# Odd layer's attention: probabilities transposed in 32-row strips, four banks at once

## The chip, the cores and the metric

The kernel runs on one core of a Trainium2 chip, in one launch. The metric is the device time of one execution in microseconds (us); lower is better. The engines are named as the profile names them: PE (TensorE's matmuls), PEld (TensorE's weight loads, which run beside its matmuls), DVE (VectorE), ACT (ScalarE), POOL (GpSimd), SP (SyncE, which issues most DMAs). "Bank" is one of the eight PSUM banks, 128 partitions x 512 float32, into which matmuls write.

## The reference, cut to what is touched

A two-layer encoder on 256 tokens of width 1024. Layer 0 (neighbourhood attention and latent attention) is not touched. Layer 1, the odd one, is attention over three groups of dilated windows, 16 heads of 64, and all three groups share one softmax by way of their denominators:

```python
for gi in range(g):                       # windows (128,1), (512,4), (2048,16)
    sc = einsum('bqhd,bqjhd->bhqj', q[gi], k_sel) * scale, masked
    e = exp(sc - max(sc)); z = sum(e)
    outs.append(einsum('bhqj,bqjhd->bqhd', e / z, v_sel)); lses.append(m + log(z))
out = sum(softmax(lses) * outs)           # then out @ w_o, residual, squared-ReLU MLP
```

## The kernel before, in words

All 256 tokens stay on the chip (two tiles of 128, `NT`); weights stream from HBM and each is split on ACT and DVE into a high and a low part (L177, L178), so that a float32 product becomes passes in the fast format (`mm2` at L187/L188, `mm3` at L181 to L183).

The odd layer works in eight units of two heads. For a unit, `qk_steps` makes queries and keys in 12 steps (three blocks `b`, two features `f`, two halves; each pair of halves fills one bank of the tag `acc`, which `joined` then empties by an ACT copy, L194, and a DVE add, L195), and `all_values` makes values in 4 steps. The attention of earlier units is put between those steps by `beside` and `burst`: the burst that belongs to unit u-1 stands after step 5 of unit u's steps, that is, right behind the product b=1, f=0, and the burst of unit 7 after step 13 of its own steps. What is left (products of units 6 and 7, transposes of unit 7) stands between the steps of the output product.

A burst for unit u has three parts, in this order:

- `mix(u-2)`: sums of values (L956, L961) into one bank, which is then split by ACT (L177) and DVE (L178).
- `turn(u-1)`: PE transposes (L942) of the probabilities `pp`, 128 queries x 384 keys for each token tile i and head j, then copies (L946) from the banks to the tile `pts`.
- `scores(u)`: L202 (two heads beside each other, each on 64 rows of the array) and L920 (four 64 x 64 products beside each other), then the softmax on DVE and ACT (L926 to L930).

Each 128-query block is transposed in two strips of 64 rows, which lie on different rows of the array and write different banks. A unit's 24 transposes stand in two groups of 12, one for each token tile: the first ahead of L202, the second, by the callback `between`, behind it.

Two pools of PSUM tags exist, `acc` and `w`, of four banks each, and each request takes the next bank in turn, so an operation that writes a bank waits until the bank's last user has been emptied. The order of instructions on each engine is fixed when the kernel is built, by a list scheduler that starts from the program's order and may move an instruction that it expects to wait; on the chip every engine works through its own list.

Of the kernel before, what the change touches and what calls it, by code (L numbers as in the profile page):

```python
# [16 lines left out]
F32 = mybir.dt.float32  # L17
# [6 lines left out]
P = 128  # L24
# [3 lines left out]
NT = T // P  # L28
# [17 lines left out]
def trunk(ctx, tc, a, out):  # L46
    nc = tc.nc
# [23 lines left out]
    def quarter_pair(name):  # L71
        return pair_tile(act, KT // 2, name, 2, "quarter")
# [5 lines left out]
    def bank(tag):  # L78
        return ps.tile([P, 512], F32, tag=tag, name=tag)
# [17 lines left out]
    ident = const.tile([P, P], F32, name="ident")  # L97
# [70 lines left out]
    def weight():  # L168

        j = state["used"]  # L170
        prefetch(j + 1, j + 1)
        prefetch(j + LOAD_AHEAD, j + SPLIT_AHEAD)
        state["used"] = j + 1
        return parts.pop(j)[1:]
# [38 lines left out]
    def soon():  # L213

        return tc.high_priority(DRAIN_PRIO)

    def tok(t):
        return slice(t * P, (t + 1) * P)
# [106 lines left out]
    def open_accs():  # L325
        return [bank("acc") for _ in range(4)]

    def onto(accs, w, c, m, first, last, fbs):

        for fb in fbs:  # L330
            cs = slice(c + fb * P, c + fb * P + P)
            o = accs[fb // 2][:, (fb % 2) * T:(fb % 2) * T + T]
            mm3(o, w[0][:, cs], w[1][:, cs], *halves(m), first and fb % 2 == 0, last and fb % 2 == 1)

    def out_steps(accs, mixed, wo, k):

        def step(fbs):
            if k // 2 not in wo:
                wo[k // 2] = weight()
            onto(accs, wo[k // 2], (k % 2) * D, mixed[k // 4][:, k % 4], k == 0, k == KT - 1, fbs)  # L340
        return [lambda fbs=fbs: step(fbs) for fbs in (range(0, 4), range(4, 8))]
# [484 lines left out]
    def odd(op, xT, s):  # L826
# [6 lines left out]
        mixed = [quarter_pair("oa"), quarter_pair("ob")]  # L833
# [72 lines left out]

        probs, turned = {}, {}

        def scores(u, d, between):

            ss = {(i, j): bank("w") for i in range(NT) for j in range(2)}
            for i in range(NT):
                two_heads([ss[i, j][:, 0:T] for j in range(2)], d["q0"], tok(i))
            between()
            for i in range(NT):
                for g in range(2):
                    for c in range(2):
                        for j in range(2):
                            pb, own = slice(64 * j, 64 * j + 64), slice(i * P + 64 * c, i * P + 64 * c + 64)
                            nc.tensor.matmul(ss[i, j][64 * c:64 * c + 64, T + 64 * g:T + 64 * g + 64], d["q12"][pb, g, own],  # L920
                                             d["k12"][pb, g, own], start=True, stop=True)
            for i in range(NT):
                for j in range(2):
                    sn, pp = scratch([384], "sn"), op.tile([P, 384], F32, tag="pp", name="pp", bufs=4)
                    mn, z, rz = (work.tile([P, 1], F32, tag=v, name=v, bufs=4) for v in ("dmn", "dz", "drz"))
                    nc.vector.tensor_tensor_reduce(out=sn, in0=ss[i, j][:, 0:384], in1=mask[:, i, :], op0=ALU.add, op1=ALU.min,  # L926
                                                   scale=-(HD ** -0.5), scalar=3e38, accum_out=mn)
                    nc.scalar.activation(pp, sn, AF.Exp, bias=mn, scale=-1.0, accum_out=z)
                    nc.vector.reciprocal(rz, z)
                    nc.scalar.activation(pp, pp, AF.Copy, scale=rz)  # L930
                    probs[u, i, j] = pp

        def turn(u, i, tag):

            pt = [bank(tag) for _ in range(2)]
            for j in range(2):
                pp = probs.pop((u, i, j))
                for b in range(3):
                    at = slice((3 * j + b) * 64, (3 * j + b) * 64 + 64)
                    for r in range(2):  # L940
                        rows = slice(64 * r, 64 * r + 64)
                        nc.tensor.transpose(pt[r][:, at], pp[rows, b * P:(b + 1) * P], ident[rows, rows])  # L942
            pts = turned[u, i] = op.tile([P, 6, P], F32, tag="pts", name="pts", bufs=2)
            with soon():
                for r in range(2):
                    nc.any.tensor_copy(out=pts[:, :, 64 * r:64 * r + 64], in_=pt[r][:, 0:384].rearrange("p (b n) -> p b n", b=6))  # L946

        def mix(u, d, out_tag):
            pvo = bank(out_tag)
            for i in range(NT):  # L950
                pts = turned.pop((u, i))
                at = i * P
                for kk in range(NT):
                    for j in range(2):
                        cs = slice(64 * j, 64 * j + 64)
                        nc.tensor.matmul(pvo[cs, tok(i)], d["v0"][:, kk, cs], pts[:, 3 * j + kk, :], start=kk == 0, stop=False)  # L956
                for c in range(2):
                    qs = slice(64 * c, 64 * c + 64)
                    for j in range(2):
                        cs = slice(64 * j, 64 * j + 64)  # L960
                        nc.tensor.matmul(pvo[cs, at + 64 * c:at + 64 * c + 64], d["v12"][:, 2 * i + c, cs], pts[:, 3 * j + 2, qs],  # L961
                                         start=False, stop=c == 1)
            with soon():
                split(*halves(mixed[u // 4][:, u % 4]), pvo[:, 0:T])

        units = [unit_tiles(0)]
        d = units[0]
        v0, v_out = value_steps(d)
        run_all(v0)
        r = [rstd(s)]  # L970
# [8 lines left out]
        def beside(main, placed):  # L979

            for i, step in enumerate(main):
                step()
                if i in placed:
                    placed[i]()

        def burst(u):

            def step():
                if u > 1:
                    mix(u - 2, units[u - 2], "acc")  # L990
                if u > 0:
                    turn(u - 1, 0, "acc")
                scores(u, units[u], lambda: turn(u - 1, 1, "acc") if u > 0 else None)
            return step

        for u in range(1, 8):
# [4 lines left out]
            beside(qk_steps(units[u]) + all_values(units[u]), placed)  # L1001
        accs, wo = open_accs(), {}

        def last_turn():
            mix(6, units[6], "w")
            for i in range(NT):
                turn(7, i, "w")

        beside([f for k in range(6) for f in out_steps(accs, mixed, wo, k)], {6: last_turn, 9: lambda: mix(7, units[7], "w")})
        return accs, out_last(accs, mixed, wo)  # L1010

    def phase(name, fn, *args):
# [3 lines left out]
    accs, last = phase("even", even)  # L1016
    xT, s = hand_over(accs, last, 1)
    accs, last, scale = phase("mlp0", mlp_between, xT, s)
    xT, s = hand_over_tokens(accs, last, 2, scale)
    accs, last = phase("odd", odd, xT, s)  # L1020
# [100 lines left out]
```

## Time and profile before

| | |
|---|---|
| runs (3) | 740.52 to 744.68 us, median 742.35 us |
| profiled execution | 740.85 us, its span 739.0 us |
| PE / PEld busy | 99% / 87% of the span |
| DVE / ACT / POOL busy | 73% / 63% / 1% |
| odd layer's units 1 to 7 (bursts) | from 354.0 us to 519.4 us; leftovers to 544.2 us |
| transposes L942 | 192 matmuls of 64 rows x 128 columns, 222 ns each in the record |

Matmuls overlap, so a record of 222 ns is a latency and not a price: what a row of transposes costs is read from the distance between starts, or from the chain of waits, which shows each group by the time that it added. A timeline row "384.55 0.53 ... x12" is a group of 12 that starts at 384.55 and whose last record ends 0.53 later. "64*128" behind a matmul is the part of the array in use, rows x columns.

### The profile page before, as it was taken

What the parts mean: (1) busy time and instruction counts of PE and PEld (TensorE: products, weight loads), DVE (VectorE), ACT (ScalarE), POOL (GpSimd) and SP (SyncE); (2) the same over time, 40 slices, a digit from 0 to 9 for tenths busy, and PEclk for the clock granted to TensorE, in tenths of its full rate; (3) what the DMA queues carried; (4) which work ended last, traced back from release to release, by engine and by line L of the source; (5) the groups of instructions that cost most, each with busy time, mean ns of one, the idle gap of its engine ahead of it and who ended that gap; (6) DMA issues with size and microseconds to landing.
All of it is one profiled execution on the core that took longest, in us unless ns stands there. A gap on an engine that the chain in (4) does not pass through costs nothing.

```text
span 739.0 us, 12836 instructions
## 1 busy us (share of the span) xinstructions
PE 729.3 (99%) x4932; PEld 641.4 (87%) x4932; DVE 538.2 (73%) x1116; ACT 463.5 (63%) x1038; POOL 6.0 (1%) x16
## 2 busy tenths in 40 slices
PE   8999999999999999999999999999999999999996
PEld 6898998888888888989999899898998888888885
DVE  6698869666666666998878888888659665665664
ACT  7689977554554556757768767776757445554541
POOL 0100000000000000000000000000000000000000
PEclk9999999999999999999999999999999999999999
DMA  8966334555555554575573665556345546455501
GB/s 288 345 207 222 116 123 163 197 202 181 178 211 180 178 184 149 200 238 200 191 247 122 200 229 169 195 173 201 128 191 194 206 171 220 168 181 200 178 20 57
DMA packets 28108, 136.89 MB, mean 185 GB/s; under 512 B 4496, under 2 KB 7056, under 8 KB 14992
## 3 DMA queue, kind: packets, MB, share of 16 engines
q1 hardware_dynamic: 27760, 135.81, 53.5%
q8 instruction: 38, 0.62, 0.3%
q10 hardware_dynamic: 288, 0.28, 0.1%
q14 instruction: 22, 0.18, 0.1%
HBM read 127.68 MB, written 1.05 MB: 174 GB/s over the span
## 4 chain that ended last, share of the span: by engine, by line
PE 89%; ACT 4%; DMA 3%; DVE 2%; issue 1%; SPq 1%; POOLq 0%; POOL 0%; ACTq 0%; DVEq 0%
PE w L187 16%; PE acc L181 13%; PE acc L182 13%; PE acc L183 13%; PE acc L187 11%; PE w L188 8%; PE acc L188 6%; PE w L761 1%; DMA raw<-in_w_v 1%; PE w L202 1%; DMA bias<-in_rpb 1%; DVE wlo L178 1%; PE acc L942 1%; PE w L729 1%; PE w L181 1%
## 5 line engine op out<-in xcount | busy, mean ns | idle before, releaser
L178 DVE TENSOR_TENSOR wlo<-raw,whi 128x512 fp32r<-128x512 f32 (+3 forms) x488 | 302.4, 665 | 67.6 <-ACT whi L177 67.2
L177 ACT CAST whi<-raw 128x512 fp32r<-128x512 f32 (+3 forms) x488 | 263.8, 602 | 80.7 <-issue 70.0
L187 PE MATMUL w<-xT,whi 128*128 128x512 f32 x512 | 179.4, 394 | 0.0
L187 PE MATMUL acc<-xT,whi 128*128 128x512 f32 x384 | 134.6, 396 | 0.0
L188 PE MATMUL w<-xT,wlo 128*128 128x256 f32 x512 | 132.8, 280 | 0.0
L187 PEld LDWEIGHTS w<-xT,whi 128*128 128x128 f32 x512 | 93.6, 187 | 18.3
L188 PEld LDWEIGHTS w<-xT,wlo 128*128 128x128 f32 x512 | 96.1, 188 | 5.5
L188 PE MATMUL acc<-xT,wlo 128*128 128x256 f32 x384 | 99.8, 280 | 0.0
L181 PE MATMUL acc<-whi,h 128*128 128x512 f32 x250 | 98.4, 393 | 0.0
L182 PE MATMUL acc<-wlo,h 128*128 128x512 f32 x250 | 97.8, 391 | 0.0
L183 PE MATMUL acc<-whi,h 128*128 128x512 f32 x250 | 97.4, 390 | 0.0
L187 PEld LDWEIGHTS acc<-xT,whi 128*128 128x128 f32 x384 | 69.8, 187 | 13.5
L194 ACT COPY up<-w 128x256 f32<-128x256 f32 x64 | 23.9, 373 | 88.6 <-PE w L187 88.6
L188 PEld LDWEIGHTS acc<-xT,wlo 128*128 128x128 f32 x384 | 72.1, 188 | 3.7
L195 DVE TENSOR_TENSOR up<-up,w 128x256 f32<-128x256 f32 x64 | 26.8, 419 | 62.9 <-ACT up L194 62.1
L181 PE MATMUL acc<-whi,xT 128*128 128x384 f32 (+2 forms) x160 | 56.1, 351 | 0.9 <-ACT whi L177 0.9
L182 PE MATMUL acc<-wlo,xT 128*128 128x384 f32 (+2 forms) x160 | 56.0, 350 | 0.4 <-DVE wlo L178 0.4
L183 PEld LDWEIGHTS acc<-whi,h 128*128 128x128 f32 x250 | 47.0, 188 | 10.2
L182 PEld LDWEIGHTS acc<-wlo,h 128*128 128x128 f32 x250 | 47.0, 188 | 9.8
L183 PE MATMUL acc<-whi,xT 128*128 128x384 f32 (+2 forms) x160 | 55.4, 346 | 0.0
L181 PEld LDWEIGHTS acc<-whi,h 128*128 128x128 f32 x250 | 46.9, 188 | 9.1
L182 PEld LDWEIGHTS acc<-wlo,xT 128*128 128x128 f32 x160 | 30.1, 188 | 3.1 <-DVE wlo L178 2.1
(201 smaller groups left out, 1009.6 us busy)
## 6 DMA issues: line engine op xcount, KB each, us to landing
raw<-in_w SPq DMA_DIRECT2D x64, 1024.0 KB, 4.8
raw<-in_w_oqk SPq DMA_DIRECT2D x24, 1024.0 KB, 5.1
raw<-in_w_ov SPq DMA_DIRECT2D x16, 768.0 KB, 4.6
sw<-qk SPq DMA_DIRECT2D x96, 64.0 KB, 3.6
raw<-in_w_qk SPq DMA_DIRECT2D x4, 1024.0 KB, 10.6
raw<-in_w_oe SPq DMA_DIRECT2D x4, 1024.0 KB, 7.7
raw<-in_w_oo SPq DMA_DIRECT2D x4, 1024.0 KB, 5.8
bias<-in_rpb SPq DMA_DIRECT2D x8, 256.0 KB, 5.3
```

The lines of the kernel that those rows point to most:

```text
L177: a = nc.scalar.copy(hi, src).ins
L178: return a, (eng or nc.vector).tensor_tensor(lo, src, hi.bitcast(F32), op=ALU.subtract).ins
L181: nc.tensor.matmul(o, sh, mh, start=first, stop=False)
L182: nc.tensor.matmul(o, sh, ml, start=False, stop=False)
L183: nc.tensor.matmul(o, sl, mh, start=False, stop=last)
L187: both = lambda: nc.tensor.matmul(o, sh, m.rearrange("p v n -> p (v n)"), start=first, stop=last)
L188: low = lambda: nc.tensor.matmul(o[:, 0:T], sl, m[:, 0, :], start=False, stop=False)
L194: nc.scalar.copy(dst, o[:, T:2 * T])
L195: nc.vector.tensor_tensor(dst, dst, o[:, 0:T], op=ALU.add)
L202: nc.tensor.matmul(o[j], qk[pb, 0, a, ts], qk[pb, 1, b, :], start=n == 0, stop=n == 2)
L729: nc.tensor.transpose(pt[:, b * P:(b + 1) * P], pp[:, b // 2, (b % 2) * P:(b % 2 + 1) * P], ident)
L761: nc.tensor.matmul(pvo[64 * j:64 * j + 64, o + own.start:o + own.stop], v[:, kk, h * 64:(h + 1) * 64], block(2 * j + kk), start=kk == 0, s ...
```

## The change

`turn` now takes a whole unit (both token tiles, both heads) at once, cuts every 128-query block into four strips of 32 rows instead of two of 64, and writes them to four banks, so a unit has 48 transposes of 32 moving columns in place of 24 of 64. They all stand between `mix` and `scores`; the callback goes. `mix` takes its bank from `w` instead of `acc`; `turn` takes all four `acc` banks. `pts` is one tile of 12 blocks in place of two of 6. The four copies of a unit move as many elements as before, in runs of 32 instead of 64. Behind the last unit, `mix(6)` and `turn(7)`, which stood together after step 6 of the output product, now stand after steps 5 and 6.

```diff
@@ -906,12 +906,11 @@
 
         probs, turned = {}, {}
 
-        def scores(u, d, between):
+        def scores(u, d):
 
             ss = {(i, j): bank("w") for i in range(NT) for j in range(2)}
             for i in range(NT):
                 two_heads([ss[i, j][:, 0:T] for j in range(2)], d["q0"], tok(i))
-            between()
             for i in range(NT):
                 for g in range(2):
                     for c in range(2):
@@ -930,25 +929,26 @@
                     nc.scalar.activation(pp, pp, AF.Copy, scale=rz)
                     probs[u, i, j] = pp
 
-        def turn(u, i, tag):
-
-            pt = [bank(tag) for _ in range(2)]
-            for j in range(2):
-                pp = probs.pop((u, i, j))
-                for b in range(3):
-                    at = slice((3 * j + b) * 64, (3 * j + b) * 64 + 64)
-                    for r in range(2):
-                        rows = slice(64 * r, 64 * r + 64)
-                        nc.tensor.transpose(pt[r][:, at], pp[rows, b * P:(b + 1) * P], ident[rows, rows])
-            pts = turned[u, i] = op.tile([P, 6, P], F32, tag="pts", name="pts", bufs=2)
+        def turn(u, tag):
+
+            pt = [bank(tag) for _ in range(4)]
+            for i in range(NT):
+                for j in range(2):
+                    pp = probs.pop((u, i, j))
+                    for b in range(3):
+                        n = (2 * i + j) * 3 + b
+                        for r in range(4):
+                            rows = slice(32 * r, 32 * r + 32)
+                            nc.tensor.transpose(pt[r][:, 32 * n:32 * n + 32], pp[rows, b * P:(b + 1) * P], ident[rows, rows])
+            turned[u] = op.tile([P, 12, P], F32, tag="pts", name="pts", bufs=1)
             with soon():
-                for r in range(2):
-                    nc.any.tensor_copy(out=pts[:, :, 64 * r:64 * r + 64], in_=pt[r][:, 0:384].rearrange("p (b n) -> p b n", b=6))
+                for r in range(4):
+                    nc.any.tensor_copy(out=turned[u][:, :, 32 * r:32 * r + 32], in_=pt[r][:, 0:384].rearrange("p (b n) -> p b n", b=12))
 
         def mix(u, d, out_tag):
             pvo = bank(out_tag)
             for i in range(NT):
-                pts = turned.pop((u, i))
+                pts = turned[u][:, 6 * i:6 * i + 6]
                 at = i * P
                 for kk in range(NT):
                     for j in range(2):
@@ -987,10 +987,10 @@
 
             def step():
                 if u > 1:
-                    mix(u - 2, units[u - 2], "acc")
+                    mix(u - 2, units[u - 2], "w")
                 if u > 0:
-                    turn(u - 1, 0, "acc")
-                scores(u, units[u], lambda: turn(u - 1, 1, "acc") if u > 0 else None)
+                    turn(u - 1, "acc")
+                scores(u, units[u])
             return step
 
         for u in range(1, 8):
@@ -1001,12 +1001,8 @@
             beside(qk_steps(units[u]) + all_values(units[u]), placed)
         accs, wo = open_accs(), {}
 
-        def last_turn():
-            mix(6, units[6], "w")
-            for i in range(NT):
-                turn(7, i, "w")
-
-        beside([f for k in range(6) for f in out_steps(accs, mixed, wo, k)], {6: last_turn, 9: lambda: mix(7, units[7], "w")})
+        beside([f for k in range(6) for f in out_steps(accs, mixed, wo, k)],
+               {5: lambda: mix(6, units[6], "w"), 6: lambda: turn(7, "w"), 9: lambda: mix(7, units[7], "w")})
         return accs, out_last(accs, mixed, wo)
 
     def phase(name, fn, *args):
```

On every engine the order is otherwise as before but for a few rows. Three places matter below.

PE at the burst in unit 1's steps, which has no `mix`: the rows behind the product L187/L188, with the waits for semaphores in brackets. Before:

```order
L187 MATMUL acc<-xT,whi 128x512
L942 MATMUL acc<-ident,pp 128x64 [waits DVE_49,Activation_49]
L942 MATMUL acc<-ident,pp 128x64 [waits DVE_49]
L942 MATMUL acc<-ident,pp 128x64 x10
L202 MATMUL w<-q_3510 128x256 x12
L942 MATMUL acc<-ident,pp 128x64 [waits DVE_49] x2
L942 MATMUL acc<-ident,pp 128x64 x10
L920 MATMUL w<-k_3512,q_3511 64x64 x16
```

The same place now:

```order
L187 MATMUL acc<-xT,whi 128x512
L942 MATMUL acc<-ident,pp 128x32 [waits DVE_49,Activation_49]
L942 MATMUL acc<-ident,pp 128x32 [waits DVE_49] x2
L942 MATMUL acc<-ident,pp 128x32 x24
L942 MATMUL acc<-ident,pp 128x32 [waits DVE_49]
L942 MATMUL acc<-ident,pp 128x32 x20
L202 MATMUL w<-q_3510 128x256 x12
L919 MATMUL w<-k_3512,q_3511 64x64 x16
```

The second group has moved ahead of L202 (L920 is now L919). The transpose that waits for DVE in the middle is the first into the fourth bank, which is the bank of the product just ahead; the scheduler has put 27 transposes of the first three strips before it, and behind it stand 9 of the fourth strip alone, then 12 in turn over all four banks. In the bursts of units 2 to 7 that wait stands at the 8th or 9th of the 48 and the rest follow in turn.

DVE behind the burst of unit 7 (L894 and L899 are the rotary embedding of this unit's keys, which L920 needs). Before:

```order
L178 TENSOR_TENSOR ob<-acc,ob 128x256
L946 COPY pts<-acc 128x6x64
L894 TENSOR_TENSOR sw<-sw,sinT 128x512
L946 COPY pts<-acc 128x6x64
L899 TENSOR_TENSOR k_5792<-r_6090,sw 128x512
```

Now:

```order
L178 TENSOR_TENSOR ob<-w,ob 128x256
L946 COPY pts<-acc 128x12x32 x2
L894 TENSOR_TENSOR sw<-sw,sinT 128x512
L899 TENSOR_TENSOR k_5907<-r_6228,sw 128x512
L925 ISA sn,dmn<-w,mask 128x384
```

Both copies now stand ahead of both steps of the keys.

PE in the output product, where `mix(6)` and `turn(7)` stood together. Before:

```order
L956 MATMUL w<-pts,v_5401 64x128 x4
L961 MATMUL w<-pts,v_5402 64x64 x4
L942 MATMUL w<-ident,pp 128x64 x15
L942 MATMUL w<-ident,pp 128x64 [waits DVE_49]
L942 MATMUL w<-ident,pp 128x64 x8
L181 MATMUL acc<-oa,whi 128x256 [waits Activation_49]
```

Now the sums stand 12 output matmuls ahead, and the transposes alone:

```order
L183 MATMUL acc<-oa,wlo 128x256
L942 MATMUL w<-ident,pp 128x32 x3
L942 MATMUL w<-ident,pp 128x32 [waits DVE_49]
L942 MATMUL w<-ident,pp 128x32 x44
L181 MATMUL acc<-oa,whi 128x256 [waits Activation_49]
```

The wait of the 16th transpose for the split of `mix(6)`'s bank has become a wait of the 4th, a step of the output product later than the sums.

## The prediction

> **What bounds the kernel now.** I read the page first, then who waits for whom on PE in the odd layer.
>
> ```profile
> PE 729.3 (99%) x4932; PEld 641.4 (87%) x4932; DVE 538.2 (73%) x1116; ACT 463.5 (63%) x1038; POOL 6.0 (1%) x16
> ...
> PE 89%; ACT 4%; DMA 3%; DVE 2%; issue 1%; SPq 1%; POOLq 0%; POOL 0%; ACTq 0%; DVEq 0%
> ```
>
> ```profile
> PE acc L181 <- ACT v L864: 0.3, 1, 0.3
> PE w L942 <- DVE ob L178: 0.2, 1, 0.2
> PE acc L942 <- DVE ob L178: 0.2, 1, 0.2
> ```
>
> PE carries 99% of the span and 89% of the chain that ended last. In the 240 us around the odd layer it waits three times, 0.7 us together, and two of these are transposes that wait for a bank. So what the change does to the time is what it does to PE's own time at eight places, and new waits for banks. DVE and ACT are behind PE nearly everywhere.
>
> **What a row of transposes costs.** The chain at one full burst (the one in unit 2's steps), then PE's timeline there, and a burst without transposes (unit 0):
>
> ```profile
> 382.75 0.44 PE acc L956 x8
> 383.19 0.23 PE acc L961 x8
> ...
> 384.71 0.37 PE acc L942 x12
> 385.08 0.62 PE w L920 x32
> ```
>
> ```profile
> 383.35 0.59 PE L942 MATMUL acc<-ident,pp 64*128 64x64 f32 x12
> 383.75 0.96 PE L202 MATMUL w<-q 64*128 64x256 f32 x12
> 384.55 0.53 PE L942 MATMUL acc<-ident,pp 64*128 64x64 f32 x12
> 385.01 0.69 PE L920 MATMUL w<-k,q 64*64 64x64 f32 x32
> ```
>
> ```profile
> 326.92 0.98 PE L202 MATMUL w<-q 64*128 64x256 f32 x12
> 327.83 0.70 PE L920 MATMUL w<-k,q 64*64 64x64 f32 x32
> ```
>
> Twelve transposes add 0.37 us, six pairs of strips: 62 ns a pair, so the two strips do run beside each other. L920 runs four beside each other: eight fours in 0.62 us, 78 ns a four with its entry and exit. L956 moves 128 columns and needs 0.44/4 = 110 ns a pair, L961 moves 64 and needs 58. So the moving side halves with the columns, and a strip of 32 should need some 30 ns. The other side is the weight load, which stays 128 columns wide. The record lengths of the loads (shortest/median/longest), and a matmul that moves a single column:
>
> ```profile
> L942 PEld LDWEIGHTS acc<-ident,pp x168: 134/139/142, 354.0 to 519.2; 64*128 64x128 f32 x168
> ...
> L956 PEld LDWEIGHTS acc<-pts,v x96: 132/137/138, 381.9 to 516.8; 128*64 128x64 f32 x96
> ...
> L249 PEld LDWEIGHTS w<-mean,squares x16: 186/190/192, 19.5 to 570.1; 128*128 128x128 f32 x16
> ```
>
> ```profile
> 129.06 0.47 PE L249 MATMUL w<-mean,squares 128*128 128x1 f32 x3
> ```
>
> L249 moves one column, its record lasts 250 ns, and three of them end 0.47 us after the first began: they repeat every 110 ns, which can only be the load. Its load record is 190, so 80 of a record is latency. By the same 80 the loads of L956 (137) take 57 and the transposes' (139) 59. That is the pitch of a pair, 62. At 64 moving columns load and moving side fall together, and the trace can't separate them; at 32 the moving side halves and the load does not. So I take **60 ns a four**: 48 transposes then cost what 24 did. The ends are 30 ns (moving side alone) and 124 (two pairs one after the other).
>
> The Trainium skill's page "TensorE: Matmul & The Clock Gate", section "LDWEIGHTS (loading the stationary operand)", says that a load costs by its columns and not by its rows, 107 ns for 128 columns. L249's 110 agrees; the transposes, 128 columns every 62 ns, do not. By that figure a four would take 107 ns and, by the count of steps below, the sum would be about 3.8 us more than mine. For its first half, that fewer rows don't make a load shorter, the run will be the test.
>
> **The change part by part.**
>
> 1. *Bursts in the steps of units 2 to 6.* Between the first transpose and L920 lie 385.01 - 383.35 = 1.66 us now. After: the group takes a first step of 0.11 (the first group above is 0.06 longer than the second, the one behind a change of the array's split) and 11 steps of 0.06, and one step more because the fourth bank starts late: 0.78 with the offsets inside a four. Then comes a change of split: the second group's last transpose starts at 384.55 + 0.53 - 0.22 = 384.86, and L920, on another split, 0.15 later, while the first group's last, at 383.72, is followed by L202, on the same split, after 0.03. Now L202 also stands on another split than the transposes, so 0.15. L202 to L920 with nothing between takes 327.83 - 326.92 = 0.91. Sum 0.78 + 0.15 + 0.91 = 1.84, so +0.18 a burst, +0.9 for five. What was saved by not splitting the group is paid by the change of split.
>
> 2. *The burst in unit 1's steps.* No `mix` stands ahead of it, and the fourth bank is that of the product just ahead. The rows of PE, then of ACT and DVE, which empty that bank:
>
> ```profile
> 354.02 0.59 PE L942 MATMUL acc<-ident,pp 64*128 64x64 f32 x12
> ...
> 355.21 0.53 PE L942 MATMUL acc<-ident,pp 64*128 64x64 f32 x12
> 355.68 0.69 PE L920 MATMUL w<-k,q 64*64 64x64 f32 x32
> ```
>
> ```profile
> 354.12 0.37 ACT L194 COPY qk<-acc 128x256 f32<-128x256 f32 x1 [0.78 <-PE acc L187]
> ```
>
> ```profile
> 354.02 0.69 DVE L893 TENSOR_TENSOR r<-qk,cosT 128x512 f32<-128x512 f32 x1
> 354.62 0.41 DVE L195 TENSOR_TENSOR qk<-qk,acc 128x256 f32<-128x256 f32 x1
> ...
> 382.96 0.42 DVE L195 TENSOR_TENSOR qk<-qk,acc 128x256 f32<-128x256 f32 x1
> ```
>
> The bank is free at 354.62 + 0.41 = 355.03. Now the second group, which uses it, starts at 355.21, behind L202, and waits for nothing. After the change the 27 transposes of the other strips end their starts at 354.02 + 0.05 + 8 x 0.06 = 354.55, and PE then stands until about 355.10 (0.07 from DVE's end to PE's start, as at 518.83 and 518.90 below). Then come nine transposes on one strip, which can't run beside each other, at 0.06 each (the row x15 below: three lone ones add 0.19), and three fours: last start 355.81. With 0.15 + 0.91, L920 starts at 356.87 against 355.68: **+1.2 us**. L202, which covered this wait, now stands behind it. In unit 2's steps the bank is free at 383.38 and the 8th transpose is due at 383.5: `mix` covers it there, as in units 3 to 6, whose L195 starts earlier still against PE.
>
> 3. *The burst of unit 7.*
>
> ```profile
> 518.90 0.59 PE L942 MATMUL acc<-ident,pp 64*128 64x64 f32 x11 [0.17 <-DVE ob L178]
> 519.41 0.44 PE L181 MATMUL acc<-whi,xT 128*128 128x384 f32 x1
> ...
> 521.17 0.69 PE L920 MATMUL w<-k,q 64*64 64x64 f32 x32
> ```
>
> ```profile
> 517.63 0.36 ACT L864 ACTIVATE v<-acc,rstd 64x128 f32<-64x128 f32 x1
> ```
>
> ```profile
> 518.41 0.42 DVE L178 TENSOR_TENSOR ob<-acc,ob 128x256 fp32r<-128x256 f32 x1 [1.35 <-ACT ob L177]
> ...
> 520.29 0.68 DVE L899 TENSOR_TENSOR k<-r,sw 128x512 f32<-128x512 f32 x1
> ```
>
> Its second group waits now for the split of `mix`'s bank, 518.83. That wait goes, since `mix` uses `w`. In its place the fourth bank is that of the values, which ACT empties until 517.99, so the 9th transpose starts at 518.06, and the fourth bank's twelve take 0.05 + 11 x 0.06: last start 518.77. L181 follows at 518.77 + 0.15 + 0.91 = 519.83, 0.4 later than now. What counts is L920, which waits for the keys (L899): both copies now stand ahead of L894 and L899 on DVE and start some 0.2 after the last transpose, at 518.98, so L899 ends some 0.2 later. L920 moves by as much, and behind it the chain through the softmax on ACT, on which PE waits at 527.14 (the 0.3 above). I take +0.3; bounds 0 and +0.6.
>
> 4. *The end.* `mix(6)` with 24 transposes, and `mix(7)` alone, from L956 to the next output product:
>
> ```profile
> 535.25 0.66 PE L956 MATMUL w<-pts,v 128*64 128x128 f32 x8
> ...
> 536.73 0.78 PE L942 MATMUL w<-ident,pp 64*128 64x64 f32 x15
> ...
> 538.25 0.39 PE L181 MATMUL acc<-oa,whi 128*128 128x256 f32 x1
> ...
> 542.76 0.66 PE L956 MATMUL w<-pts,v 128*64 128x128 f32 x8
> ...
> 544.25 0.39 PE L181 MATMUL acc<-ob,whi 128*128 128x256 f32 x1
> ```
>
> Now 3.00 us, with a wait for the split (0.2 in the waits, some 0.4 with the restart). After: `mix(6)` alone 1.49, another entry and exit 0.19, transposes 0.72 + 0.15: 2.55, so -0.45. The wait is covered by the output step that now stands between.
>
> 5. *Copies.* Four of the same 384 elements a unit, costed at nothing: they run beside L202 and L920 (1.5 us), and the next product needs only the first bank. If runs of 32 were slower this would still cover them. No DMA moves.
>
> Sum: 0.9 + 1.2 + 0.3 - 0.45 = +1.95 us. On the profiled execution (740.85, span 739.0 and 1.85 around it) 742.8; that one is 1.5 below the median of the runs, so on the median **744.3 us**.
>
> **The rivals.**
>
> *The moving side sets the pace*: 30 ns a four. What speaks for it is 110 and 58 for 128 and 64 columns; against it the load of 59. About 80 steps of fours are on the path (five bursts, unit 7 and the end with 11 each, unit 1 with 3), so -2.4, and the nine lone ones give -0.3: 1.95 - 2.7 = -0.7, 741.6 us. Even so the waits and changes of split eat most of the gain.
>
> *Only two strips run beside each other* (slower): nothing in this trace shows four row strips at once; L920's four lie on two row halves and two column halves. At 124 ns a four 80 steps cost 80 x 0.064 = 5.1 more: +7.1, 749.4 us. It decides from where 80 steps give 3.7 - 1.95, that is above 82 ns a four. Against it stands L920, whose four loads of four banks fit in 78.
>
> *Every matmul needs a slot of its own.* L920's 32 in 0.62 us are 19 ns each, L942's 12 in 0.37 us are 31; at the middle, 25, a four takes 100 and 80 x 0.04 = 3.2 come on top: 747.5 us. Against it speaks that L920 already comes closer, so its chance is small. The Trainium skill, same page, section "Wait — 56ns, not 53.3ns?", has a rule of this kind: starts never come closer than about 25 ns, however little is moved; L920's 19 ns does not agree.
>
> *The waits for banks are otherwise*: if the scheduler's nine lone transposes or the stall in unit 1 are hidden, -1.2; if units 2 to 6 also stand for the fourth bank, up to 0.5 each. This is the spread of my own case: 742.8 to 746.
>
> **Chances.** Forecast 0.6, moving side 0.2, two at a time 0.1, own slots 0.05, anything else 0.05. A measurement of this kernel tells about 0.5%, 3.7 us, from no change: below 738.65 or above 746.05. Faster has no mechanism here, 0.04; slower gets two at a time, own slots and the upper edge of my case, 0.2; the rest, 0.76, is the same. For 8 in 10 the range reaches down to the moving side's case with the scatter of a run, and up to the slots': 740.6 to 747.6.
>
> **What the profile after would show.** The group x48 at a burst lasting 0.78 + 0.2 in the timeline (0.45 + 0.2 if the moving side bounds, 1.5 and more if two at a time); 0.15 between its last start and L202; in unit 1's steps a group of 27, a gap of about half a microsecond that ends with DVE L195, and lone transposes; no wait of L942 for `ob`; at the end 2.55 us in two pieces. The forecast fails if a four's pitch is not near 60, or if the fourth bank is waited for at every burst.

## The result, and the profile after

| | before | after |
|---|---|---|
| median of all runs | 741.22 us (740.45 to 744.68, 13 runs) | 745.12 us (743.88 to 749.56, 13 runs) |
| ratio | | 1.0051, 95% interval 1.0036 to 1.0065 |
| profiled execution, span | 740.85, 739.0 us | 743.92, 742.1 us |
| first L202 of unit 0 to the output product behind the last `mix` ("the odd layer" below) | 217.33 us | 220.50 us |

The forecast of 744.3 us lies 0.8 us from the median. As a difference it does less well: +1.95 us was forecast, the two profiled executions lie 3.07 us apart, and the medians 3.9. The forecast started from the median of three runs, 742.35 us; over 13 runs the median is 741.22, 1.1 us lower. That the time came out so near is in part luck.

Two lines of the page after, the busy times and the chain that ended last:

```profile
PE 731.6 (99%) x5124; PEld 642.6 (87%) x5124; DVE 538.5 (73%) x1116; ACT 462.5 (62%) x1038; POOL 6.1 (1%) x16
...
PE 86%; ACT 5%; DVE 3%; DMA 3%; issue 1%; SPq 1%; POOLq 0%; POOL 0%; ACTq 0%; DVEq 0%
```

PE is as busy as before, but its share of the chain fell from 89% to 86%: somewhere in the chain other engines now end last. PE's waits around the odd layer (in total, times, longest) say where:

```profile
PE acc L942 <- DVE qk L195: 0.9, 2, 0.6
PE acc L942 <- ACT v L864: 0.4, 1, 0.4
```

All of PE's waits there now belong to transposes, for a bank of `acc`. PE's timeline at three bursts: unit 1's, unit 3's, and unit 4's.

```profile
353.93 0.75 PE L942 MATMUL acc<-ident,pp 32*128 32x32 f32 x27
355.01 0.92 PE L942 MATMUL acc<-ident,pp 32*128 32x32 f32 x21 [0.33 <-DVE qk L195]
355.86 0.97 PE L202 MATMUL w<-q 64*128 64x256 f32 x12
356.76 0.69 PE L919 MATMUL w<-k,q 64*64 64x64 f32 x32
...
414.29 0.95 PE L942 MATMUL acc<-ident,pp 32*128 32x32 f32 x48
415.16 0.97 PE L202 MATMUL w<-q 64*128 64x256 f32 x12
416.07 0.69 PE L919 MATMUL w<-k,q 64*64 64x64 f32 x32
...
443.75 0.37 PE L942 MATMUL acc<-ident,pp 32*128 32x32 f32 x7
444.72 0.92 PE L942 MATMUL acc<-ident,pp 32*128 32x32 f32 x41 [0.61 <-DVE qk L195]
445.57 0.97 PE L202 MATMUL w<-q 64*128 64x256 f32 x12
446.47 0.69 PE L919 MATMUL w<-k,q 64*64 64x64 f32 x32
```

From the first transpose to L919 unit 3 takes 416.07 - 414.29 = 1.78 us (1.66 before), unit 1 takes 2.83, unit 4 takes 2.73. In unit 3 nothing is waited for. In unit 4 seven transposes run, and the eighth, the first into the fourth bank, stands until DVE has emptied the product just ahead (L195). The bracket counts 0.61 us as idle, from the end of the seventh's record; from the first start of the 48 to the last it is 0.95 us more than in unit 3 (1.68 and 0.73). The other bursts: 2.19, 1.98 and 1.79 us in units 2, 5 and 6.

The chain through unit 4's stall, in order of time, shows what the bank waited for. Before, every piece of the chain in the same stretch was PE's.

```profile
433.91 2.87 ACT whi L177 x6
436.81 0.36 ACT v L863
...
438.32 1.14 ACT whi L177 x2
439.49 0.39 ACT qk L194
439.90 0.31 DVE qk L195
440.24 1.29 DVE wlo L178 x2
441.53 0.33 DVE qk L195
441.86 1.87 DVE wlo L178 x4
443.73 0.60 DVE r L893
444.33 0.34 DVE qk L195
444.72 0.92 PE acc L942 x41
```

In this chain one of ACT and DVE works at any time for 11 us, and L195 comes last: they run late, and the late bank is where PE feels it. Matched with the same instructions before, PE is 1.7 us later here, DVE 3.1. DVE fell behind in the burst before: against the same instructions before it is 1.6 us late just ahead of L894 and 3.7 at L894, which waits for the DMA that swaps the halves of queries (`sw`). Two rows of DVE's timeline there, then DVE's waits at L894 over units 0 to 7, after and, in the second row, before:

```profile
417.06 0.08 DVE L925 DVE_READ_ACCUMULATOR2_ANT dmn<- 128x1 f32 x1
419.19 0.69 DVE L894 TENSOR_TENSOR sw<-sw,sinT 128x512 f32<-128x512 f32 x1 [2.04 <-DMA sw<-qk]
```

```profile
DVE sw L894 <- DMA sw<-qk: 7.6, 7, 2.0
```

```profile
DVE sw L894 <- DMA sw<-qk: 3.1, 4, 1.6
```

### The profile page after: what moved, and what is told of

Same layout as the page of the kernel before. It is cut to its first block, busy times and chain, and to the rows that moved or that the text cites. A ratio compares the mean times of both kernels' runs of the same rounds, so it can differ in the third digit from the quotient of the medians.

```text
span 742.1 us, 13215 instructions
## 1 busy us (share of the span) xinstructions
PE 731.6 (99%) x5124; PEld 642.6 (87%) x5124; DVE 538.5 (73%) x1116; ACT 462.5 (62%) x1038; POOL 6.1 (1%) x16
## 4 chain that ended last, share of the span: by engine, by line
PE 86%; ACT 5%; DVE 3%; DMA 3%; issue 1%; SPq 1%; POOLq 0%; POOL 0%; ACTq 0%; DVEq 0%
PE w L187 16%; PE acc L181 14%; PE acc L182 14%; PE acc L183 13%; PE acc L187 9%; PE w L188 8%; PE acc L188 4%; ACT whi L177 2%; DVE wlo L178 2%; DMA sw<-qk 1%; PE w L202 1%; PE w L761 1%; DMA raw<-in_w_v 1%; PE w L729 1%; PE acc L942 1%
## 5 line engine op out<-in xcount | busy, mean ns | idle before, releaser
L187 PE MATMUL w<-xT,whi 128*128 128x512 f32 x512 | 179.4, 394 | 0.0
L187 PE MATMUL acc<-xT,whi 128*128 128x512 f32 x384 | 134.6, 397 | 0.0
L188 PE MATMUL w<-xT,wlo 128*128 128x256 f32 x512 | 132.8, 280 | 0.0
L187 PEld LDWEIGHTS w<-xT,whi 128*128 128x128 f32 x512 | 93.6, 187 | 18.3
L188 PEld LDWEIGHTS w<-xT,wlo 128*128 128x128 f32 x512 | 96.1, 188 | 5.5
L188 PE MATMUL acc<-xT,wlo 128*128 128x256 f32 x384 | 99.8, 280 | 0.0
L187 PEld LDWEIGHTS acc<-xT,whi 128*128 128x128 f32 x384 | 69.8, 187 | 13.5
L188 PEld LDWEIGHTS acc<-xT,wlo 128*128 128x128 f32 x384 | 72.1, 188 | 3.7
L195 DVE TENSOR_TENSOR up<-up,w 128x256 f32<-128x256 f32 x64 | 26.9, 420 | 62.8 <-ACT up L194 62.0
```

The costliest lines, as they stand in the source:

```text
L187: both = lambda: nc.tensor.matmul(o, sh, m.rearrange("p v n -> p (v n)"), start=first, stop=last)
L188: low = lambda: nc.tensor.matmul(o[:, 0:T], sl, m[:, 0, :], start=False, stop=False)
L195: nc.vector.tensor_tensor(dst, dst, o[:, 0:T], op=ALU.add)
```

## The experiments

The theory from these rows, called LATE BANK: of the 3.2 us, about half is PE waiting for the fourth bank in units 2, 4 and 5, because DVE is late; the rest are the terms forecast. Rivals: STRIPS (four strips of 32 rows simply cost more) and ORDER (standing ahead of L202 delays the scores). Later runs add two questions: what sets a four's price, and why DVE is late. In all tables "burst" is the time from the first transpose (or L202, where it comes first) to L919/L920.

### The same kernel again; strips of 64 rows; the transposes behind L202; the end alone

> The changed kernel once more, nothing edited, for a second trace. Three accounts of the 3.1 us between the two profiled executions. LATE BANK: the first transpose into the fourth bank waits until DVE has emptied the product just ahead (L195), and how late that is hangs on when the swapped queries and keys land by DMA (L894). Then unit 1's burst takes 2.8 us again from the first transpose to L919 (1.66 before), and in units 2 to 6 the stalls fall on other bursts and have other sizes than in the first trace (0.4, 0, 0.95, 0.2, 0 us), each where DVE runs late. STRIPS: four strips of 32 rows cost more than two of 64; then every burst is longer by the same amount, in both traces. ORDER: standing all ahead of L202 delays the scores and the softmax; then the extra time lies behind the bursts. Time by all three: 744 to 747 us, ratio 1.004 to 1.006.

> The changed kernel with strips of 64 rows: 24 transposes a unit, two banks for each token tile, still all ahead of L202, mix still in w, end as changed. LATE BANK: the transposes stand on the same split of the array as L202, and the fourth bank is first needed 0.4 us after the first transpose in place of 0.1: a burst without a stall 1.67 us; unit 1 some 2.35 (1.08 until the bank is free, less 0.4); the other stalls 0.3 shorter each. Sum 0.7 + about 0.6 + 0.3 (unit 7) - 0.45 (end) = about +1.2 us, ratio 1.0015. STRIPS: all of the loss goes and the end's gain stays, -0.3 us, ratio 0.9995. ORDER: the loss stays, +3 us or more, ratio 1.004 to 1.005.

```diff
-                        for r in range(4):
-                            rows = slice(32 * r, 32 * r + 32)
-                            nc.tensor.transpose(pt[r][:, 32 * n:32 * n + 32], pp[rows, b * P:(b + 1) * P], ident[rows, rows])
+                        at = slice((n % 6) * 64, (n % 6) * 64 + 64)
+                        for r in range(2):
+                            rows = slice(64 * r, 64 * r + 64)
+                            nc.tensor.transpose(pt[2 * i + r][:, at], pp[rows, b * P:(b + 1) * P], ident[rows, rows])
```

> The changed kernel with the 48 transposes of 32 rows behind L202 in place of ahead of it (L202, transposes, L920). Same strips, same banks, same end. LATE BANK: L202 takes 0.9 us first, so the bank is free when it is needed (unit 1: 1.08 after L202's start against 0.95 + 0.1, so 0.1 of waiting at most; none in units 2 to 6). The changes of split stay, so 1.78 us from L202 to L920 in each burst, +0.12 each for six. With +0.3 for unit 7 and -0.45 at the end: +0.6 us, ratio 1.001. STRIPS: stays at +3 us, ratio 1.004. ORDER: the scores still stand behind all transposes, so +3 us too, or more where L920 is meant.

```diff
                 two_heads([ss[i, j][:, 0:T] for j in range(2)], d["q0"], tok(i))
+            between()
...
-                    turn(u - 1, "acc")
-                scores(u, units[u])
+                scores(u, units[u], lambda: turn(u - 1, "acc") if u > 0 else None)
```

> The kernel before with two pieces of the change alone: mix takes its bank from w in every unit, and at the end mix(6) stands after step 5 and the transposes of unit 7 after step 6 of the output product. Strips of 64 rows in two groups, as before. All three accounts: bursts of 1.66 us as before; the end takes 2.55 us in two pieces in place of 3.00, -0.45 us; the wait of unit 7's second group for the split of mix's bank (0.17 us) goes, but keys bound that place. Sum -0.45, ratio 0.9994, too little for the times to show; the trace decides. If mix in w is a cost of its own (bursts longer, or new waits of L202 for a bank of w), the bursts show it and the time is +0.5 us or more.

```diff
-                    mix(u - 2, units[u - 2], "acc")
+                    mix(u - 2, units[u - 2], "w")
...
-            mix(6, units[6], "w")
...
-{6: last_turn, 9: ...}
+{5: lambda: mix(6, units[6], "w"), 6: last_turn, 9: ...}
```

| | ratio to before, 95% | bursts of units 1 to 6, us | odd layer, us |
|---|---|---|---|
| before | | 1.66 each | 217.33 |
| after | 1.0051 (1.0036 to 1.0065) | 2.83, 2.19, 1.78, 2.73, 1.98, 1.79 | 220.50 |
| again | 1.0065 (1.004 to 1.0089) | 2.83, 1.99, 2.05, 2.47, 3.25, 1.79 | 222.34 |
| strips64 | 1.0004 (0.9985 to 1.0024) | 2.34, then 1.66 each | 217.44 |
| between | 1.013 (1.0106 to 1.0154) | 1.92, 2.63, 3.56, 2.41, 2.57, 2.42 | 226.18 |
| end_only | 1.0018 (1.0008 to 1.0029) | 1.66, then 1.92 each | 218.58 |

*Again* came out as LATE BANK said: unit 1 the same to the hundredth, the rest on other bursts. Unit 5, 1.98 us in the first trace, is the worst here. The row of DVE in the burst ahead of it shows the wait, and matched with the kernel before DVE goes there from 2.5 to 5.0 us late:

```profile
449.92 0.69 DVE L894 TENSOR_TENSOR sw<-sw,sinT 128x512 f32<-128x512 f32 x1 [2.57 <-DMA sw<-qk]
```

```profile
473.94 0.37 PE L942 MATMUL acc<-ident,pp 32*128 32x32 f32 x7
475.43 0.92 PE L942 MATMUL acc<-ident,pp 32*128 32x32 f32 x41 [1.12 <-DVE qk L195]
```

STRIPS falls as the main cause: a price that lies in the strips can't change from one execution to the next by 1.3 us in one burst.

*Strips64* keeps order, banks and end, and its odd layer is 0.11 us over before, so ORDER falls too. Its first burst and its second on PE's timeline:

```profile
356.80 0.90 PE L943 MATMUL acc<-ident,pp 64*128 64x64 f32 x17
357.87 0.40 PE L943 MATMUL acc<-ident,pp 64*128 64x64 f32 x4 [0.18 <-DVE qk L195]
...
359.14 0.69 PE L919 MATMUL w<-k,q 64*64 64x64 f32 x32
...
386.81 0.96 PE L943 MATMUL acc<-ident,pp 64*128 64x64 f32 x24
387.58 0.96 PE L202 MATMUL w<-q 64*128 64x256 f32 x12
388.47 0.69 PE L919 MATMUL w<-k,q 64*64 64x64 f32 x32
```

Unit 1 waits for the same bank and takes 2.34 us; 2.35 was expected from when the bank comes free. In units 2 to 6 no stall is left at all, better than expected (+0.1 and not +1.2 us): DVE is on time in this kernel: L195 ends 0.47 us ahead of the first transpose in every one of these units, and L894 waits 1.4 us in all (7.6 in the changed kernel). So 32-row strips, or the 24 further transposes a unit that come with them, which this run takes away as well, bring two things: a change of split and a late DVE.

*Between* went against the forecast (+8.9 us and not +0.6). A row shows one reason: with `mix` in `w`, L202's fourth bank is the one that `mix` has just filled, and the transposes that used to cover its split now stand behind.

```profile
414.30 0.98 PE L202 MATMUL w<-q 64*128 64x256 f32 x9
416.44 0.61 PE L202 MATMUL w<-q 64*128 64x256 f32 x3 [1.17 <-DVE oa L178]
```

*End_only* shows the same wait in small: with `mix` in `w` L202 takes 0.95 us (0.80 before) and the second group 0.57 (0.46), +0.26 a burst. That eats the end's gain, and by its interval this kernel is slightly slower than before.

### Behind L202 with mix in acc; the end alone with mix in acc

> The changed kernel with the 48 transposes behind L202, as in the run before, and mix's bank taken from acc again, so that L202 no longer has to wait for mix's split (that wait, 0.65 to 1.8 us a burst, decided the run before). LATE BANK: the third bank is now the product's, free 0.5 us before mix ends in units 2 to 6 and 1.08 us after L202's start in unit 1; the fourth is mix's, split by about 0.95 us after L202's start; transposes start 0.91 after it. So at most 0.1 to 0.2 of waiting a burst, 1.78 to 1.95 us from L202 to L920 against 1.66: +0.7 to +1.7 for six; unit 7 up to +0.3, end -0.45: +0.5 to +1.6 us in the odd layer, ratio 1.001 to 1.002. STRIPS (four strips of 32 rows cost more by themselves, no wait in it): +3 us or more, ratio 1.004. ORDER: +3 us or more.

> The kernel before with one piece of the change: mix(6) after step 5, the transposes of unit 7 after step 6 of the output product. mix stays in acc up to unit 7. Expected: bursts 1.66 us as before (with mix in w they took 1.91 in units 2 to 6); the end -0.45 us; ratio 0.9994, which only the trace can tell. If mix in w was not the cause of the 1.91, it comes back here: +1 us, ratio 1.001.

Both undo one line of the runs above:

```diff
-                    mix(u - 2, units[u - 2], "w")
+                    mix(u - 2, units[u - 2], "acc")
```

*Between_acc*: ratio 1.0128 (1.0102 to 1.0154), bursts 1.92, 1.86, 1.86, 3.12, 3.29, 1.85, odd layer 227.73 us. Expected were 1.78 to 1.95, and four of six have it, but units 4 and 5 stall and even products wait (27.20 us for the 144 products behind unit 4's burst, 25.56 where nothing waits). The forecast had overlooked DVE's order, which this edit also changes: the scheduler put L894, which waits for the swap, ahead of the softmax's first step, so in unit 3 the whole softmax stood behind a landing for 2.98 us. The experiment is confounded and says nothing against ORDER by itself; it does show what a late DVE costs.

*End_acc*: ratio 0.9993 (0.9982 to 1.0003), bursts 1.66 each, odd layer 216.82 us, 0.51 less than before; 0.45 was expected. Three rows of its end:

```profile
534.19 0.66 PE L956 MATMUL w<-pts,v 128*64 128x128 f32 x8
...
537.30 0.96 PE L942 MATMUL w<-ident,pp 64*128 64x64 f32 x24
538.19 0.39 PE L181 MATMUL acc<-oa,whi 128*128 128x256 f32 x1
```

The transposes take 0.89 us alone where they took 1.52 behind `mix`. This piece beats the changed kernel. Over the kernel before, its half microsecond stands in one trace of each, and the interval of the times includes no change.

### Without the swap

> The changed kernel without the DMAs that swap the halves of queries and keys (L891, L892): L894 reads the unswapped tile, so the rotary embedding is left out in part; DVE has the same count of steps and never waits for a landing. LATE BANK: the stalls of units 2 to 6 come from DVE being late after L894's wait, so they go: 0.88 us for T48 in each (0.88 to 2.34 in the two traces of the changed kernel); unit 1 keeps its 1.93, which hangs on no DMA. From L202 of unit 0 to the last mix some 1.5 to 4 us less than in the changed kernel, at most 2 us over the same edit of the kernel before. STRIPS and ORDER: the bursts stay as long as with the swap, 3 us or more over the same edit of the kernel before.

> The same edit on the kernel before, as the measure for the run above. All accounts: DVE's waits for the swap (3.1 us in units 1 to 7) were not on PE's path, so bursts stay 1.66 us and the odd layer within 0.5 us of the kernel before: ratio 0.998 to 1.001.

```diff
-                for r in range(0, P, 64):
-                    nc.sync.dma_start(sw[r:r + 32], s[r + 32:r + 64])
-                    nc.sync.dma_start(sw[r + 32:r + 64], s[r:r + 32])
...
-                nc.vector.tensor_tensor(sw, sw, sinT...
+                nc.vector.tensor_tensor(sw, s, sinT...
```

On the changed kernel: ratio 1.0036 (1.002 to 1.0052), odd layer 219.39 us; on the kernel before: 1.0004 (0.9991 to 1.0017), 217.84 us, but with bursts of 1.77 us in units 2 to 6 where 1.66 was expected. The difference of the odd layers is 1.55 us, under the 2 expected; the medians lie 2.5 us apart, and 3.9 with the swap. Every stall of units 2 to 6 is gone; they take 1.80 or 1.81 us, as here in unit 2:

```profile
385.25 0.94 PE L939 MATMUL acc<-ident,pp 32*128 32x32 f32 x48
386.13 1.01 PE L202 MATMUL w<-q 64*128 64x256 f32 x12
387.06 0.69 PE L916 MATMUL w<-k,q 64*64 64x64 f32 x32
```

Unit 1 still stalls, as expected, and for longer (3.17 us), since DVE's order differs and L195 ends there 0.34 us later against PE. That is why the gain over the changed kernel, 1.1 and 2.95 us against its two traces, begins below the 1.5 to 4 expected. So the stalls of units 2 to 6 go when nothing waits for the swap. DVE's order differs in these kernels throughout, so the pair alone doesn't separate the landing from the order. The jumps of DVE's lateness at L894, with DVE's order there unchanged, do.

### What sets a four's price

> The changed kernel with the weight load of each transpose cut to 64 of the 128 keys; the moving side stays 32 columns, the count 48. The other 64 keys are left out (the first 64 are copied twice, by twice as many copies on ACT and DVE, so the kernel's time is no measure; the pitch of the fours is). LOAD: a four falls from 62 ns to some 31 to 40 ns, T48 from 0.87 to 0.5 to 0.6 us where it does not wait. SLOTS (each transpose takes an issue slot of 15 ns, whatever it loads): 62 ns as now. MOVING: 62 ns as now, since the moving side is unchanged.

```diff
-nc.tensor.transpose(pt[r][:, 32 * n:32 * n + 32], pp[rows, b * P:(b + 1) * P], ident[rows, rows])
+nc.tensor.transpose(pt[r][0:64, 32 * n:32 * n + 32], pp[rows, b * P:b * P + 64], ident[rows, rows])
```

> The kernel before with each pair of transposes issued twice into the same place: 48 transposes a unit, as in the changed kernel, but as 24 pairs of 64 rows and not 12 fours of 32. LOAD (each pair or four costs the 62 ns of its 128-column weight load): every group of 12 grows from 0.39 to 0.76 us, a burst from 1.66 to 2.40; six bursts, +4.5 us, the end +0.75, unit 7 0 to 0.75: +5.2 to +6 us, ratio 1.007 to 1.008. STRIPS: if pairs were not the limit but single transposes were (31 ns each), the 48 here would cost what the 48 there do, 0.75 to 0.88 us in all, which this kernel gives as the price of 24. FETCH: with 48 more PE instructions a unit the fetches drift against the bursts as in the changed kernel, so some swaps land late here too (a gap over 1 us in two or more of units 1 to 6, against one before).

```diff
-                    for r in range(2):
+                    for r in (0, 1, 0, 1):
```

The unstalled group in unit 2 of cols64, on PE's timeline; then its load records (shortest/median/longest), and behind them those of the changed kernel:

```profile
386.18 0.60 PE L942 MATMUL acc<-ident,pp 32*64 32x32 f32 x48
386.71 1.09 PE L202 MATMUL w<-q 64*128 64x256 f32 x12
```

```profile
L942 PEld LDWEIGHTS acc<-ident,pp x336: 102/108/116, 356.0 to 526.1; 32*64 32x64 f32 x168
```

```profile
L942 PEld LDWEIGHTS acc<-ident,pp x336: 132/137/140, 353.9 to 522.0; 32*128 32x128 f32 x168
```

With half the columns loaded the records are 29 ns shorter, 48 transposes take 0.53 us and not 0.88, and the starts of one strip repeat every 33 ns, not 62. Same count and same moving side, so LOAD holds, and SLOTS and MOVING fall.

*Doubled_before*: each doubled group takes 0.77 us from its first start to the next product's (the row below runs to the end of the last record), for 0.39 with half as many, an unstalled burst 2.42 (2.40 expected): the price of a pair is right.

```profile
355.18 0.96 PE L942 MATMUL acc<-ident,pp 64*128 64x64 f32 x24
```

The time is not: ratio 1.0191 (1.0176 to 1.0206), where 1.007 to 1.008 was expected. In this kernel the scheduler put L894 ahead of the second copy and of the whole softmax, DVE waits 19.8 us there in all, and units 3 to 6 take 3.0 to 3.3 us. FETCH missed here as well: no swap at the burst in units 1 to 6 has a gap over 0.7 us, where gaps over 1 us were expected in two or more. DVE at unit 2's burst:

```profile
386.40 0.55 DVE L946 COPY pts<-acc 128x384 f32<-128x384 f32 x1
390.69 0.69 DVE L894 TENSOR_TENSOR sw<-sw,sinT 128x512 f32<-128x512 f32 x1 [3.74 <-DMA sw<-qk]
```

### Why the swap lands late

The trace's DMA packets around the wait of 2.04 us shown above (start, end, queue, bytes), with the swap's last packets and the only one on queue 8:

```
416.282 417.471 q8 16384
416.847 416.987 q1  2048
417.468 417.695 q1  2048
417.681 417.906 q1  2048
417.901 418.122 q1  2048
418.108 418.272 q1  2048
```

Queue 8 brings instructions. The swap's other 124 packets have ended by 416.99 us; the last four start when the instruction packet ends and follow one another, which looks like a queue behind it on one DMA engine; the trace doesn't name the engine of a packet. The landing of one of the four transfers then came 1.56 us after that of the one ahead; where no instruction packet is near, the gap of these swaps is 0.2 to 0.4 us.

A unit has 488 records of matmuls and loads on PE before and 536 after, 24 more transposes with a load each. Some two packets fall in a unit. In units 2 to 6 one of them came 5.0, 4.6, 4.2, 4.1 and 4.6 us behind the first transpose before, when the swap had landed; after, at 2.9, 2.0, -1.4, -1.9 and -6.2 us, earlier from unit to unit, and so on the swap or, it may be, on the weights ahead of it, which no run separates. To test this I moved all packets:

> The kernel before with 30 short warm-up matmuls at the start in place of 8 long ones (44 more PE instructions in the same time), every other instruction and its order unchanged. FETCH: packets of 16 KB that bring PE's instructions hold one DMA engine for 1.0 to 1.3 us, and a swap whose packets queue behind one lands that much later; in the kernel before they lie 4.1 to 5.0 us behind the first transpose of units 2 to 6, just after the swap has landed, in the changed kernel on the swap (2.0 to 2.9 us behind it in units 1 to 3). 44 instructions earlier they come about 2 us behind it here: in several of units 2 to 6 a landing 1.0 to 1.6 us behind the one ahead of it (0.2 to 0.4 without a fetch), and DVE's waits at L894 grow from 3.1 us to 5 us or more. The bursts stay 1.66 us, or nearly, since the bank has slack there: ratio 0.999 to 1.003. CHANCE (landings vary by themselves): the same gaps as in the kernel before.

> The same edit on the changed kernel. FETCH: the stalls of the 48 transposes move with the fetches: other units stall than in the two traces (0.4, 0, 0.95, 0.2, 0 and 0.2, 0.27, 0.7, 1.5, 0 us in units 2 to 6), and each swap with a landing gap over 1 us lies on a fetch; which way the sum goes hangs on where all twelve fetches fall, 742.5 to 747 us. Unit 1 keeps 1.93. CHANCE: the stalls fall as in the two traces, or without any fetch beside them.

```diff
-            nc.tensor.matmul(idle, warm[:, 0:P], warm, start=True, stop=True)
+            nc.tensor.matmul(idle[:, 0:P], warm[:, 0:P], warm[:, 0:P], start=True, stop=True)
-    keep_warm(8)
+    keep_warm(30)
```

*Shift_before* missed its numbers: ratio 1.0008 (0.9991 to 1.0025), bursts 1.66, but the packets of units 3 to 6 stayed at 4.0 to 4.4 us, only unit 2's came to 2.0 and held nothing up, and unit 1's went from 2.7 to -2.1. There the gap fell from 1.48 to 0.20 us, and DVE's waits at L894 from 3.1 to 0.9 us in place of rising. So only unit 1's packet could be steered, and why the others stay in place in the kernel before is open.

*Shift_after*: ratio 1.0039 (1.0025 to 1.0054), bursts 2.82, 1.79, 2.38, 1.79, 1.79, 1.78, odd layer 219.44 us. Unit 1 is as ever; of the stalls in units 2 to 6 one is left, in unit 3, behind a swap of unit 2 with a packet on it (gap 1.60 us). Unit 1's packet moved to -2.1 us here too, and its gap fell from 1.46 to 0.20:

```profile
415.26 0.37 PE L942 MATMUL acc<-ident,pp 32*128 32x32 f32 x7
415.88 0.93 PE L942 MATMUL acc<-ident,pp 32*128 32x32 f32 x41 [0.26 <-DVE qk L195]
```

With 44 instructions more at the start of the program, over 300 us earlier, the stalls are 0.6 us in place of 1.6 (2.6 in the second trace). The two traces of the changed kernel differ by as much, so the sum proves little; where the gaps fall says more. Each unit has three swaps. Over the twelve traces with the swap, twelve of the 72 swaps at the bursts of units 1 to 6 have a gap over 0.9 us; each has an instruction packet that began 1.9 to 3.1 us behind the burst's first row. Seven such packets left no gap of this size, and among the 53 swaps without one the largest gap is 0.53. So for these swaps the packet goes with the gap and is not sufficient. It is not the whole of DVE's lateness: in the second trace's unit 4, where L894 waits 2.57 us, the largest gap is 0.39, and in unit 5 the second swap has a gap of 0.95 to 1.2 us without a packet in five traces (0.6 to 0.7 is usual for second swaps). Why the swap lands late is thus shown in part.

## Why the prediction was right or wrong

| step | forecast | measured |
|---|---|---|
| 1. units 2 to 6, change of split | +0.18 each, +0.9 | +0.12 each, +0.6 |
| 1. units 2 to 6, wait for the fourth bank | 0 | +0.41, 0, +0.95, +0.2, 0: +1.6 |
| 2. unit 1 | +1.19 | +1.17 |
| 3. unit 7, `mix` to L919 | +0.3 | +0.31 (5.65 against 5.34) |
| 4. the end, L919 of unit 7 to the product behind `mix(7)` | -0.45 | -0.45 (22.63 against 23.08) |
| sum | +1.95 | +3.2 |

- *The price of a four*, 60 ns between ends of 30 and 124: right, and for the reason given. It is the 128-column load: 62 ns a four, 33 with 64 columns. The Trainium skill's rule that a load costs by its columns and not by its rows (page "TensorE: Matmul & The Clock Gate", section "LDWEIGHTS (loading the stationary operand)") agrees for columns by the 33, and for 32 and 64 rows by the equal 62 ns of fours and pairs. Against it stand the 128 rows of L249, at 110 ns for as many columns; the 107 ns that its formula gives for 128 columns fits L249 and doesn't hold for these transposes. The rival "moving side" is out by cols64, "two at a time" by the 62 ns, and "own slots" by 48 starts in 0.41 us in cols64, 9 ns each.
- *The change of split*: right in kind. Unit 3's 1.78 and unit 6's 1.79 us show +0.12, since the group takes 0.73 us from first start to last and not 0.78: the extra step that I had put in for the late fourth bank isn't there, and the 0.15 and 0.91 behind it are as counted.
- *Unit 1*: right in its parts, 27 transposes, the stop for DVE L195, the rest, and L202 behind it. Strips64's 2.34 us confirms the bank's time.
- *Units 2 to 6, where the step failed*: "`mix` covers it there, as in units 3 to 6, whose L195 starts earlier still against PE". The sentence reads one execution's DVE times as fixed. In that trace L195 ended between 0.02 us behind and 0.47 us ahead of the first transpose, so the margin was half a microsecond, while the same trace showed L894 waiting up to 1.6 us for a DMA on the same engine. In the two traces of the changed kernel L195 ends up to 0.92 and 1.43 us behind it. The rival I had priced at "up to 0.5 each" was the right one and too small, by half in unit 4 and by two thirds in unit 5 of the second trace.
- *Unit 7 and the end*: right in size in the first trace; for unit 7 the second gives +1.1 in place of +0.31, so the close match is partly chance. At the end the two pieces and the vanished wait are as counted. At unit 7 the 9th transpose waited for the values' bank (ACT L864), as forecast, and the late keys set L919.
- *Copies at nothing*: right; no row of PE's waits names a copy, and one takes 553 ns on DVE as before, on ACT 483 (479 before), so the runs of 32 don't make DVE late.

The term that was put at nothing, the fourth bank in units 2 to 6, is 1.6 of the 3.2 us in the first trace, and 2.6 of 5.0 us in the second (222.34 against 217.33), where unit 7 adds 1.1 (6.44 against 5.34). The forecast's own sign, the fourth bank waited for at every burst, did not come: three of units 2 to 6 wait in the first trace, four in the second. That these waits also make the changed kernel's runs spread from 743.9 to 749.6 us fits, but was not tried.

## What to carry to other kernels

Taking all buffers of a pool at once spends slack that doesn't show as a wait: before costing that at nothing, find the engine that frees the last buffer, and compare its margin with the longest wait that this engine has anywhere in its loop, not with its own time in one trace. Cutting the moving side of small matmuls gains nothing once the load of the stationary side sets the pace, so look first at which of the two a pitch follows. An edit of the busiest engine's work can also move another engine's waiting instruction ahead of that engine's own work, as it did L894 in two experiments here (between_acc and doubled_before); both came out over 8 us above their forecasts.

## What the runs showed of the hardware that was not expected

- An instruction packet of 16 KB takes 0.9 to 1.75 us in the traces of the odd layer. In the rows above four small packets of a swap start one after the other from the moment it ends, while others ran beside it; in twelve swaps one landing came 1.0 to 1.9 us behind the one ahead of it, in place of 0.2 to 0.5. With 536 PE records a unit in place of 488 these packets fall earlier from unit to unit.
- Four transposes of 32 rows do run beside each other, 62 ns for four with 128 columns loaded and 33 ns with 64. The Trainium skill's page "TensorE: Matmul & The Clock Gate", section "Wait — 56ns, not 53.3ns?", has starts never closer than about 25 ns; 15 and 9 ns a start, on strips of 32 rows, do not agree.
- A change of the array's split costs PE about 0.12 us each time (0.15 from start to start where 0.03 stands on the same split; 0.12 in cols64).
